# Gate products of the gated recurrence as 64-row products of a half tile each, run for two tiles or for one, some of them in the next pass; weight splits put between the square root and the exponentials

## The chip, the cores and the metric

The kernel runs on one core of a Trainium2 chip. The time is the device time of one execution in microseconds (us), the median over runs. Engines are named as in the profile: PE (matrix products), PEld (PE's weight loads), DVE, ACT, POOL, and the queues SPq and ACTq that issue transfers.

## The reference

One layer of a hybrid decoder for 512 positions and a width of 1024, in float32: a projection of the normalised input, three token mixers beside each other, their gated sum, and a feed-forward block. The change is in the third mixer, the gated recurrence, whose gates are products with 64x64 blocks, one for each of 16 heads:

```python
xc = lax.conv_general_dilated(xr, conv_w[:, None, :], ...) + conv_b
xh = xc.reshape(B, S, RNN_HEADS, RNN_HEAD_DIM)          # 16 heads of 64
r = jax.nn.sigmoid(jnp.einsum('bshi,hio->bsho', xh, w_a).reshape(B, S, RNN_WIDTH) + b_a)
i = jax.nn.sigmoid(jnp.einsum('bshi,hio->bsho', xh, w_x).reshape(B, S, RNN_WIDTH) + b_x)
log_a = -LRU_C * r.astype(jnp.float32) * jax.nn.softplus(-lam.astype(jnp.float32))
a = jnp.exp(log_a)
b_in = jnp.sqrt(-jnp.expm1(2.0 * log_a)) * (i * xc).astype(jnp.float32)
_, h = lax.associative_scan(combine, (a, b_in), axis=1)  # h[t] = a[t] h[t-1] + b_in[t]
return h.astype(xr.dtype) * jax.nn.gelu(gate)
```

## The kernel before, in words

**Numbers in two parts.** Every operand of a product is split into a rounded part `hi` and a remainder `lo` (`split`, L131 on ACT and L136 on DVE), and a product is three products: hi·hi, hi·lo, lo·hi. A *pass* (`passes`, L263) is one tile of 128 output columns for all 512 positions: eight blocks of 128 rows by three, 24 products, into one bank of PSUM. Its weights come by SPq into `raw` (two buffers), are split into `hi` and `lo` (three buffers each), and are fetched two passes ahead (`unit`).

**The recurrence in two halves.** Its 1024 channels are eight tiles of 128, four in each half `b`. For a tile, `xr_tile` makes a pass, then the convolution (`xc`: L499 on ACT, L501 three times on DVE), splits it into `ch` and `cl`, and then makes the gate products (L509): for each of the two gates three products of 128x512, with a weight tile of 128x128 that holds two 64x64 blocks on its diagonal and zeros beside them. Both gates go to banks with the tag `tr`. ACT reads each with one instruction (L511 the sigmoid into `r`, L514 a tanh into `ti`). `rec_batch` then makes for four tiles a tanh (L523), one square root (L524), four exponentials (L530), and on DVE the products and the scan (L539 to L542). The square root and the exponentials need other tables of ACT, each loaded before it. `rec_out` multiplies with the gelu of another pass (`rg_tile`) and splits the outcome into `ych` and `ycl`.

**The order.** The code runs generators: `run` takes the passes one by one; what a tile does behind its pass comes some steps later, in the midst of the following pass; a side generator (`rec_batch`, `rec_out`) is stepped now and then. What is still outstanding is finished at the end of a `run`. A scheduler then puts each engine's instructions in an order, and each engine works through its own in that order. `compress` and `hidden` are the first layer of the compressed keys (L784, 64 products), `c_gate` a pass whose outcome ACT takes with a tanh into `merged` (L1179). Behind these comes `c_stage`: for each pair of output tiles, seven products of blocks (L1273, 84 instructions of 128x256), which go by turns to two banks that ACT has to empty (L1277, L1281, L1284, L1289, L1296) before the next product of that bank may begin. They need sums of the recurrence's outcome and of the weights `raw`, made on DVE and ACT just before.

Of the kernel before, what the change touches and what calls it, by code (L numbers as in the profile page):

```python
# [33 lines left out]
NK = 8  # L34
# [18 lines left out]
def hybrid_block(ctx: ExitStack, tc: tile.TileContext, A, out):  # L53
# [84 lines left out]
    res = {}  # L138
# [4 lines left out]
    def w_in(*tiles):  # L143
# [311 lines left out]


    wab = {}

    def start_wab():
        wab["raw"] = slab("wabr", tag="s1", shape=(2, NK, 128))  # L460
# [14 lines left out]
    yc = {}  # L475
    rec = {}
# [11 lines left out]
    def xr_tile(b, c):  # L488
        if c == 0:
            res["late"] = res["raw"]  # L490
            rec[b] = dict(R=slab("r", tag="y" if b else "m"), GG=slab("gg", tag="m"), TI=slab("ti", tag=("s0", "s1")[b]))
        k = 4 * b + c
        ps = bank("mm")
        yield from matrix(ps, hh, hl)
        xc = row("xc")

        def cw(w):
            return vec[:, V_CW + 8 * w + k:V_CW + 8 * w + k + 1]
        res["xc"] = SC.activation(xc, ps, AF.Identity, scale=cw(3), bias=vec[:, V_CB + k:V_CB + k + 1])  # L499
        for i in (1, 2, 3):  # L500
            res["cv"] = V.scalar_tensor_tensor(xc[:, i:], ps[:, :S - i], cw(3 - i), xc[:, i:], op0=OP.mult, op1=OP.add)  # L501
        yield
        ch, cl = row("ch", F32R), row("cl", F32R)
        split(xc, ch, cl)
        yield 4
        for g, dst in ((0, "R"), (1, "TI")):
            pg = bank("tr")
            for t, (w, x) in enumerate((("hi", ch), ("hi", cl), ("lo", ch))):
                PE.matmul(pg, wab[w][:, g, k, :], x, start=(t == 0), stop=(t == 2))  # L509
            if g == 0:  # L510
                SC.activation(rec[b]["R"][:, c, :], pg, AF.Sigmoid, bias=vec[:, V_BA + k:V_BA + k + 1])  # L511
            else:
                ti = rec[b]["TI"][:, c, :]
                last = SC.activation(ti, pg, AF.Tanh, scale=0.5, bias=half[:, 0, k:k + 1])  # L514
                res["ti"] = last, V.scalar_tensor_tensor(ti, ti, 1.0, xc, op0=OP.add, op1=OP.mult)
            yield

    def rec_batch(b):
        r = rec[b]
        r["T"] = slab("t", tag="s2")  # L520
        for c in range(4):
            k = 4 * b + c
            SC.activation(r["T"][:, c, :], r["R"][:, c, :], AF.Tanh, scale=sp4[:, k:k + 1])  # L523
        root = SC.activation(r["T"], r["T"], AF.Sqrt, scale=1.0 / 16)  # L524

        def exps(cs):
            with tc.issue_after(root.ins):
                for c in cs:
                    a = r["R"][:, c, :]
                    SC.activation(a, a, AF.Exp, scale=spm8[:, 4 * b + c:4 * b + c + 1])  # L530

        exps((0, 1) if b else range(4))
        yield
        for c in range(4):
            k = 4 * b + c
            if b and c == 0:
# [170 lines left out]
    def gate_tile():  # L707
# [8 lines left out]
        SC.activation(s[:64], ps[64:], AF.Copy)  # L716
        V.tensor_add(s[:64], s[:64], ps[:64])
        SC.activation(s[:64], s[:64], AF.Sigmoid)
        yield
        pt = bank("tr")  # L720
        for c in range(4):
            PE.transpose(pt[:, c * 64:(c + 1) * 64], s[:64, c * 128:(c + 1) * 128], ident[:64, :64])
# [1323 lines left out]
            close(0, 3, 2 - n, part)  # L2046


    def run(main, side=None, rate=1.0):


        credit = 0.0
        late = []
        for m in main:
            for w in m:
                for x in late:
# [10 lines left out]
                    if next(side, 0) == 0:  # L2067
                        side = None
            credit += rate
        for _, m in late:  # L2070
            for _ in m:
                pass
        if side is not None:
            for _ in side:
                pass

    def seq(*gens):
        for g in gens:
# [49 lines left out]
    def both_out():  # L2128

        batch = rec_batch(1)  # L2130
        next(batch)
        yield
        yield from after(res["ti"], rec_out(0))
        yield from batch
        yield from rec_out(1)

    def inputs(tile, kv):

        for w in tile:
# [126 lines left out]
```

## Time and profile before

| what | value |
|---|---|
| median of 3 runs | 1090.13 us (1089.93 to 1090.33) |
| the profiled execution's own time | 1089.44 us |
| its span, first to last instruction | 1087.7 us |
| mean granted clock of PE | 0.998 |
| PE busy | 1078.3 us, 99% of the span |
| DVE busy | 883.0 us, 81% |
| ACT busy | 661.7 us, 61% |
| gate products, from first to last | 66.8 to 145.7 us |
| first L1273 | 211.3 us |

The profile comes from one execution. A product's time in it is from its start to its modelled end; products overlap, so what one takes away from the next is read from the distance of their starts. The chain of waits follows the work that ended last back to its start. A shape such as 128*128 behind a product is the part of the array that it uses, 64*128 a product over 64 rows.

### The profile page before, as it was taken

To read this page: it belongs to the slowest core of one execution; us is meant where nothing else is said; L and a number is where in the kernel's file an instruction comes from. 1 tells how busy PE (TensorE), PEld (TensorE's weight loads), DVE (VectorE), ACT (ScalarE), POOL (GpSimd) and SP (SyncE) were. 2 spreads that over 40 slices of the span, in tenths; PEclk is the share of its full clock that TensorE was granted. 3 is DMA by queue.
4 is the path that set the end of the run, shared out by engine and by line. 5 is a ranking of instruction groups with operands and counts; after the bars stand their busy time and mean duration, and the time that the engine had idled before them with its cause. 6 is when DMAs were issued, how large, how long until landed. Compare 5 with 4: busy or idle time off the path is not lost.

```text
span 1087.7 us, 16765 instructions
## 1 busy us (share of the span) xinstructions
PE 1078.3 (99%) x6450; PEld 948.5 (87%) x6450; DVE 883.0 (81%) x1557; ACT 661.7 (61%) x1210; POOL 29.0 (3%) x41
## 2 busy tenths in 40 slices
PE   9999999999999999999999999999999999999997
PEld 7888888999889888898888889988999999998886
DVE  6967779669675899998998887876988888889675
ACT  6757574454444676876777655555666666667542
POOL 0000000000000000000000000000000000022200
PEclk9999999999999999999999999999999999999999
DMA  8332325430322221102111134271323322378902
GB/s 312 113 99 82 97 86 204 178 98 20 117 78 78 78 59 39 59 20 79 59 39 59 58 118 136 72 257 39 117 78 117 117 104 97 130 227 202 191 20 97
DMA packets 35312, 115.07 MB, mean 106 GB/s; under 512 B 3584, under 2 KB 3984, under 8 KB 34336
## 3 DMA queue, kind: packets, MB, share of 16 engines
q1 hardware_dynamic: 28496, 97.01, 27.0%
q0 software_dynamic: 5152, 11.09, 5.0%
q10 hardware_dynamic: 1584, 5.90, 1.4%
q8 instruction: 50, 0.82, 0.3%
q14 instruction: 30, 0.25, 0.1%
HBM read 111.89 MB, written 2.10 MB: 105 GB/s over the span
## 4 chain that ended last, share of the span: by engine, by line
PE 97%; DVE 1%; DMA 0%; issue 0%; ACT 0%; DVEq 0%; SPq 0%; ACTq 0%
PE mm L263 37%; PE mm L1755 18%; PE mm L1273 7%; PE mm L1894 6%; PE mm L625 4%; PE mm L1509 4%; PE o L992 4%; PE sc L954 3%; PE tr L979 3%; PE tr L1894 3%; PE mm L870 2%; PE tr L784 1%; PE tr L509 1%; PE mm L1611 1%; PE tr L685 1%; PE tr L892 1%
## 5 line engine op out<-in xcount | busy, mean ns | idle before, releaser
L263 PE MATMUL mm<-hh,hi 128*128 128x512 f32 x504 | 199.5, 396 | 0.0
L263 PE MATMUL mm<-hh,lo 128*128 128x512 f32 x504 | 197.4, 392 | 0.0
L263 PE MATMUL mm<-hl,hi 128*128 128x512 f32 x504 | 196.9, 391 | 0.0
L136 DVE TENSOR_TENSOR lo<-raw,hi 128x1024 fp32r<-128x1024 f32 (+1 forms) x105 | 121.0, 1153 | 38.4 <-ACT hi L131 35.3
L131 ACT ACTIVATE hi<-raw 128x1024 fp32r<-128x1024 f32 (+1 forms) x105 | 105.3, 1003 | 46.5 <-PE mm L263 17.3
L263 PEld LDWEIGHTS mm<-hh,lo 128*128 128x128 f32 x504 | 94.6, 188 | 19.7
L263 PEld LDWEIGHTS mm<-hl,hi 128*128 128x128 f32 x504 | 94.7, 188 | 18.4 <-issue 0.2
L263 PEld LDWEIGHTS mm<-hh,hi 128*128 128x128 f32 x504 | 94.7, 188 | 18.0 <-PE mm L1273 0.2
L960 ACT ACTIVATE P<-P,ast 128x128 f32<-128x128 f32 (+3 forms) x128 | 70.7, 555 | 23.1 <-DVE ast L958 22.5
L958 DVE CUSTOM_DVE_ANT_0 P<-sc,mask 128x128 f32<-128x128 f32 (+3 forms) x128 | 57.9, 484 | 8.2 <-PE sc L954 7.3
L131 ACT ACTIVATE ph<-tr 128x512 fp32r<-128x512 f32 x80 | 46.9, 592 | 25.9 <-PE tr L979 24.0
L136 DVE TENSOR_TENSOR pl<-tr,ph 128x512 fp32r<-128x512 f32 x80 | 54.4, 685 | 2.7 <-PE o L992 0.9
L954 PE MATMUL sc<-K,q 128*128 128x512 f32 (+2 forms) x192 | 51.0, 368 | 0.0
L1755 PE MATMUL mm<-t,hi 128*128 128x256 f32 x288 | 50.7, 276 | 0.0
L1894 PE MATMUL mm<-hi,u 128*128 128x512 f32 x160 | 50.1, 389 | 0.0
L979 PE MATMUL tr<-ident,P 128*128 128x128 f32 x320 | 48.7, 273 | 0.0
L979 PEld LDWEIGHTS tr<-ident,P 128*128 128x128 f32 x320 | 39.0, 140 | 9.8 <-DVE pl L136 1.0
L136 DVE TENSOR_TENSOR lo<-bs,hi 128x1024 fp32r<-128x1024 f32 x28 | 34.1, 1220 | 11.6 <-ACT hi L131 11.6
L1755 PEld LDWEIGHTS mm<-t,hi 128*128 128x128 f32 x288 | 43.4, 188 | 0.0
L1755 PE MATMUL mm<-fh,hi 128*128 128x256 f32 x144 | 40.0, 278 | 0.0
L1755 PE MATMUL mm<-fh,lo 128*128 128x256 f32 x144 | 39.8, 276 | 0.0
L1755 PE MATMUL mm<-fl,hi 128*128 128x256 f32 x144 | 39.8, 276 | 0.0
(489 smaller groups left out, 2896.6 us busy)
## 6 DMA issues: line engine op xcount, KB each, us to landing
raw<-in_w_in SPq DMA_DIRECT2D x64, 512.0 KB, 3.5
rawp<-in_w_fi SPq DMA_DIRECT2D x20, 1024.0 KB, 5.1
bs<-in_w_fo POOLq DMA_DIRECT2D x20, 512.0 KB, 8.1
raw<-in_w_br SPq DMA_DIRECT2D x14, 512.0 KB, 3.6
w<-in_cw ACTq DMA_DIRECT2D x4, 1024.0 KB, 6.7
raw<-in_w_o SPq DMA_DIRECT2D x8, 512.0 KB, 4.1
bs<-in_w_fo SPq DMA_DIRECT2D x8, 512.0 KB, 8.0
raw<-in_w_v SPq DMA_DIRECT2D x6, 512.0 KB, 4.9
```

Source lines behind the costliest of these rows:

```text
L131: res["hi"] = SC.activation(hi, src, AF.Copy)
L136: res["lo"] = V.tensor_sub(lo, src, f32(hi))
L263: res["mm"] = PE.matmul(ps[:m, n0:n1], w[:, k * 128:k * 128 + m], x[k][:, n0:n1], start=(t == 0), stop=(t == 3 * NK - 1))
L625: res["mm"] = PE.matmul(b[c], x[k][:, c * 128:(c + 1) * 128], w[:, kk * 512:kk * 512 + 512], start=(k == 0 and t == 0), stop=(k == NK - 1 ...
L954: PE.matmul(ps[:, :w * n].rearrange("p (b n) -> p b n", b=w), lhs, K[:, i, brs[0]:brs[-1] + 1, :n], start=(i == 0), stop=(i == 1))
L958: V.tensor_tensor_reduce(out=t, in0=ps[:, b * n:b * n + n], in1=mask[0][:, S - n:], scale=-0.125, scalar=3.0e38, op0=OP.add, op1=OP.min, a ...
L960: SC.activation(t, t, AF.Exp, scale=-1.0, bias=st[:, 0, j, b:b + 1], accum_out=st[:, 1, j, b:b + 1])
L979: PE.transpose(pt[:, j * 128:(j + 1) * 128], self.part(j, br)[:, kt * 128:(kt + 1) * 128], ident)
L992: PE.matmul(po, VV[:, kt, g % 2, br].rearrange("p i d -> p (i d)"), x, start=(br == 0 and kt == 0 and t == 0), stop=(br == 1 and kt == a a ...
L1273: res["mm"] = PE.matmul(ps, u[:, k * 128:k * 128 + 128], v[:, k], start=(start and k == t == 0), stop=(k == 3 and t == 2), skip_group_chec ...
L1755: res["mm"] = PE.matmul(ps, w[:, k * 128:k * 128 + 128], x[:, k], start=(start and k == t == 0), stop=(k == 3 and t == 2), skip_group_chec ...
L1894: PE.matmul(ps, a, b, start=id(ps) not in begun, stop=i == len(ops) - 1, skip_group_check=True)
```

## The change

**Smaller products.** The weight tiles of the gates no longer hold zeros: for each half of 64 channels the blocks of both gates stand beside each other (64 rows, 128 columns), so that one product of 64 rows by 128 columns gives both gates of a half tile. For a tile these are two halves by three products, six instructions as before. The two halves use different halves of the array's rows and go to different banks, tag `mm`. In the first half of the recurrence the products of two tiles are issued together, 12 in a run; in the second half those of the first two tiles are, and those of the third and fourth stand alone, 6 in a run. In both halves the last of them come in the midst of the pass that follows (`keep`: `run` hands on what is outstanding instead of finishing it).

**ACT.** Each gate of each tile is now read by two instructions of 64 partitions. In each half the tanh of the last tiles comes behind the square root. The exponentials come two by two, and the split of a weight is put between the root and them.

**Order of passes.** `cmp_tile(2)` stands in the place of the first `rg_tile` of the second half, which moves behind; the first half's `rec_out` moves forward into the second `run`; the second `c_gate` moves ahead of `hidden(first)`. `w_in` lists the weights accordingly.

```diff
-    w_in(*range(T_XR + 1, T_XR + 8, 2), T_CMP + 1, *range(T_XR + 8, T_XR + 16, 2), *range(T_XR + 9, T_XR + 16, 2),
-         T_CMP + 2, T_CMP + 3)
+    w_in(*range(T_XR + 1, T_XR + 8, 2), T_CMP + 1, *range(T_XR + 8, T_XR + 16, 2), T_CMP + 2, *range(T_XR + 9, T_XR + 16, 2),
+         T_CMP + 3)
...
+    ends = slice(0, 64), slice(64, 128)
...
-        hi = slab("wabh", F32R, "wab", (2, NK, 128), 48)
-        lo = slab("wabl", F32R, "wab", (2, NK, 128), 48)
+        hi = slab("wabh", F32R, "wab", (NK, 128), 48)
+        lo = slab("wabl", F32R, "wab", (NK, 128), 48)
...
-        for k in range(0, NK, 2):
-            split(raw[:, :, k:k + 2], hi[:, :, k:k + 2], lo[:, :, k:k + 2])
-            yield
+        for o in ends:
+            for i in range(2):
+                g = slice(64 * i, 64 * i + 64)
+                split(raw[o, i, :, o], hi[o, :, g], lo[o, :, g])
+                yield
...
-        yield 4
-        for g, dst in ((0, "R"), (1, "TI")):
-            pg = bank("tr")
-            for t, (w, x) in enumerate((("hi", ch), ("hi", cl), ("lo", ch))):
-                PE.matmul(pg, wab[w][:, g, k, :], x, start=(t == 0), stop=(t == 2))
...
+        rec[b]["x"] = rec[b].get("x", []) + [(k, xc, ch, cl)]
+        yield (5 - b) if c == 3 else 3
+        if c in ((0, 2), (0,))[b]:
+            return
+        two = rec[b].pop("x")
+        pg = [[bank("mm") for _ in ends] for _ in two]
+        for t in range(3):
+            for i, (k, xc, ch, cl) in reversed([*enumerate(two)]):
+                w, x = (("hi", ch), ("lo", ch), ("hi", cl))[t]
+                for n, own in enumerate(ends):
+                    with tc.issue_after(res["gate"].ins) if t or n or not i else nullcontext():
+                        res["gate"] = PE.matmul(pg[i][n], wab[w][own, k, :], x[own], start=(t == 0), stop=(t == 2))
+        yield
...
+            if k % 4 == 3:
+                r["root"] = SC.activation(r["T"], r["T"], AF.Sqrt, scale=1.0 / 16)
...
-        exps((0, 1) if b else range(4))
+        exps((0, 1))
...
-    run(xr_tiles(0, gate_tile()))
-    tiles = xr_tiles(1, rg_tile(1, 0))
-    run(four(rg_tile, 0) + [cmp_tile(1)] + tiles[:4], rec_batch(0), 0.45)
...
+    late = run(xr_tiles(0, gate_tile()), keep=True)
+    tiles = xr_tiles(1, cmp_tile(2))
...
+    late = run(four(rg_tile, 0) + [cmp_tile(1)] + tiles[:4], first_half(), 0.45, late, True)
...
-    run([tiles[4], *(rg_tile(1, c) for c in range(1, 4)), cmp_tile(2), inputs(cmp_tile(3), 0),
-         behind(c_gate(0), "x0", "x1"), hidden(first), inputs(c_gate(1), 1)],
-        both_out(), 0.45)
+    run([tiles[4], *four(rg_tile, 1), inputs(cmp_tile(3), 0),
+         c_gate(0), behind(c_gate(1), "x0", "x1"), inputs(hidden(first), 1)],
+        second_half(), 0.45, late)
```

**The first gate products on PE.** Before, they stand between the second and the third pass of the recurrence; `tr_710` and `tr_719` are the two gates of the first tile, `ch_670` and `cl_671` its convolved input in two parts.

```order
L263 MATMUL mm_674<-hh_134,lo_598 128x512
L509 MATMUL tr_710<-ch_670,wabh_529 128x512
L509 MATMUL tr_710<-cl_671,wabh_529 128x512
L509 MATMUL tr_710<-ch_670,wabl_530 128x512
L509 MATMUL tr_719<-ch_670,wabh_529 128x512
L509 MATMUL tr_719<-cl_671,wabh_529 128x512
L509 MATMUL tr_719<-ch_670,wabl_530 128x512
L263 MATMUL mm_725<-hh_133,hi_637 128x512
```

In the changed kernel they stand 18 products into the third pass (`mm_714`), for two tiles; `mm_738` and `mm_739` are the two halves of the first tile, `mm_740` and `mm_741` those of the second.

```order
L263 MATMUL mm_714<-hh_134,lo_638 128x512
L519 MATMUL mm_740<-ch_710,wabh_529 128x512
L519 MATMUL mm_741<-ch_710,wabh_529 128x512
L519 MATMUL mm_738<-ch_670,wabh_529 128x512
L519 MATMUL mm_739<-ch_670,wabh_529 128x512
L519 MATMUL mm_740<-ch_710,wabl_530 128x512
...
L519 MATMUL mm_740<-cl_711,wabh_529 128x512
...
L519 MATMUL mm_739<-cl_671,wabh_529 128x512
L263 MATMUL mm_714<-hh_134,hi_637 128x512
```

The products of two tiles moved together and one pass later, and neighbours in the row belong to different halves of the rows.

**ACT where `c_stage` begins.** Before, `t` are the sums of the recurrence's outcome, `hi_1749` and `hi_1767` sums of weights, `merged` the tanh of the last pass ahead of L1273, `r_273` and `r_274` what empties the two banks of L1273, and `hi_1863` the weights of the first pass behind.

```order
L131 ACTIVATE t_1757<-ti_1073 128x1024
L131 ACTIVATE hi_1749<-raw_1667 128x1024
L131 ACTIVATE hi_1767<-raw_1668 128x512
L793 ACTIVATE chid_1702<-chid_1702 128x2x124
L1179 ACTIVATE merged_1571<-mm_1789 128x512
L1277 ACTIVATE r_273_1817<-mm_1815 128x256
L1281 ACTIVATE r_274_1818<-mm_1816 128x256
L1284 ACTIVATE r_273_1817<-mm_1815 128x256
L131 ACTIVATE hi_1863<-raw_1861 128x1024
```

In the changed kernel `mm_1805` is that last pass, `t_1773`, `hi_1765` and `hi_1783` are the sums, and `hi_1879` and `hi_1936` the weights of the two passes behind.

```order
L1208 ACTIVATE merged_1595<-mm_1805 128x512
L131 ACTIVATE t_1773<-ti_1079 128x1024
L1306 ACTIVATE r_273_1833<-mm_1831 128x256
L131 ACTIVATE hi_1765<-raw_1683 128x1024
L131 ACTIVATE hi_1783<-raw_1684 128x512
L1313 ACTIVATE r_273_1833<-mm_1831 128x256
...
L1310 ACTIVATE r_274_1834<-mm_1832 128x256
...
L1318 ACTIVATE r_274_1834<-mm_1831 128x256
L131 ACTIVATE hi_1879<-raw_1877 128x1024
L1325 ACTIVATE r_274_1834<-mm_1831 128x256
L131 ACTIVATE hi_1936<-raw_1934 128x1024
```

The last of the sums and the weights that belong to them now stand behind `merged` and behind the first emptying of a bank, and `hi_1936` behind the last one.

**PE at the same place.** Before, the seven products go to the banks `mm_1815` and `mm_1816` in long turns of 8 to 15 instructions, and the pass behind them follows undivided.

```order
L1273 MATMUL mm_1815<-ych_1336,lo_1715 128x256
L1273 MATMUL mm_1816<-ych_1584,a12h_1731 128x256
...
L1273 MATMUL mm_1816<-ych_1336,lo_1750 128x256
L1273 MATMUL mm_1815<-t_1740,hi_1714 128x256 x2
...
L1273 MATMUL mm_1815<-t_1764,a22l_1709 128x256
L263 MATMUL mm_1942<-hh_133,hi_1863 128x512
L263 MATMUL mm_1942<-hl_135,hi_1863 128x512
L263 MATMUL mm_1942<-hh_133,lo_1864 128x512
```

In the changed kernel the banks are `mm_1831` and `mm_1832`, and `mm_1958` and `mm_2013` the two passes behind.

```order
L1302 MATMUL mm_1832<-ych_1569,a12l_1748 128x256
L1302 MATMUL mm_1831<-t_1756,hi_1730 128x256 x2
...
L1302 MATMUL mm_1831<-t_1756,lo_1731 128x256
L1302 MATMUL mm_1831<-t_1773,hi_1783 128x256 x2
...
L1302 MATMUL mm_1831<-t_1780,a22l_1725 128x256
L263 MATMUL mm_1958<-hh_133,hi_1879 128x512
L263 MATMUL mm_1958<-hl_135,hi_1879 128x512
L263 MATMUL mm_2013<-hh_133,hi_1936 128x512
L263 MATMUL mm_1958<-hh_133,lo_1880 128x512
```

Three instead of 15 instructions of the other bank stand between the first product of `mm_1831` and its second, none between its second (`t_1756`) and its third (`t_1773`), and one instruction of the pass `mm_2013` has moved into the pass `mm_1958`.

More of the change, by code (lines that the diff above doesn't have):

```diff
@@ L502, in xr_tile @@
         yield
-        ch, cl = row("ch", F32R), row("cl", F32R)
+        ch, cl = row("ch", F32R, "tg"), row("cl", F32R, "q32")
         split(xc, ch, cl)
-        yield 4
-        for g, dst in ((0, "R"), (1, "TI")):
-            pg = bank("tr")
-            for t, (w, x) in enumerate((("hi", ch), ("hi", cl), ("lo", ch))):
[L509 to L515, printed above, removed]
-            yield
+        rec[b]["x"] = rec[b].get("x", []) + [(k, xc, ch, cl)]
@@ new lines, in xr_tile, with act @@
+        yield
+        r = rec[b]
+        def act(out, part, k, own, n):
+            if part == 0:
+                return SC.activation(out[own], n[:64], AF.Sigmoid, bias=vec[own, V_BA + k:V_BA + k + 1])
+            return SC.activation(out[own], n[64:], AF.Tanh, scale=0.5, bias=half[own, 0, k:k + 1])
+        for i, (k, xc, ch, cl) in enumerate(two):
+            for n, own in enumerate(ends):
+                act(r["R"][:, k % 4, :], 0, k, own, pg[i][n])
+        if c < 3:
+            yield
+        else:
+            r["T"] = slab("t", tag="s2")
+            for j in range(4):
+                SC.activation(r["T"][:, j, :], r["R"][:, j, :], AF.Tanh, scale=sp4[:, 4 * b + j:4 * b + j + 1])
@@ new lines, in xr_tile @@
+        for i, (k, xc, ch, cl) in enumerate(two):
+            if k % 4 == 3:
+                r["root"] = SC.activation(r["T"], r["T"], AF.Sqrt, scale=1.0 / 16)
+            ti = r["TI"][:, k % 4, :]
+            for n, own in enumerate(ends):
+                with tc.issue_after(r["root"].ins) if "root" in r else nullcontext():
+                    last = act(ti, 1, k, own, pg[i][n])
+            res["ti"] = last, V.scalar_tensor_tensor(ti, ti, 1.0, xc, op0=OP.add, op1=OP.mult)
+            if c == 1:
+                yield
@@ L518, in rec_batch @@
     def rec_batch(b):
+        while "root" not in rec.get(b, ()):
+            yield
+        yield
         r = rec[b]
[L520 to L524, printed above, removed]
+        ahead = (r["root"], res["hi"])
         def exps(cs):
-            with tc.issue_after(root.ins):
+            with tc.issue_after(ahead[0].ins), tc.issue_after(ahead[1].ins):
@@ L535, in rec_batch @@
             k = 4 * b + c
-            if b and c == 0:
+            if c == 0:
                 exps((2, 3))
@@ L718, in gate_tile @@
         SC.activation(s[:64], s[:64], AF.Sigmoid)
-        yield
+        yield 2
         pt = bank("tr")
@@ L2046, in down, with run @@
             close(0, 3, 2 - n, part)
-    def run(main, side=None, rate=1.0):
+    def run(main, side=None, rate=1.0, late=None, keep=False):
         credit = 0.0
-        late = []
+        late = late or []
         for m in main:
@@ L2069, in run @@
             credit += rate
-        for _, m in late:
-            for _ in m:
+        while late and not keep:
+            for _ in late.pop(0)[1]:
                 pass
@@ L2075, in run @@
                 pass
+        return late
     def seq(*gens):
@@ L2124, in hybrid_block, with first_half, second_half @@
     run([v_half(0), v_half(1), cmp_tile(0)], seq(norm(), load_wab()))
-    run(xr_tiles(0, gate_tile()))
-    tiles = xr_tiles(1, rg_tile(1, 0))
-    run(four(rg_tile, 0) + [cmp_tile(1)] + tiles[:4], rec_batch(0), 0.45)
[L2128 to L2134, printed above, removed]
+    late = run(xr_tiles(0, gate_tile()), keep=True)
+    tiles = xr_tiles(1, cmp_tile(2))
+    def first_half():
+        yield from rec_batch(0)
+        while 1 not in rec:
+            yield
+        yield from rec_out(0)
+    def second_half():
+        yield from rec_batch(1)
         yield from rec_out(1)
+    late = run(four(rg_tile, 0) + [cmp_tile(1)] + tiles[:4], first_half(), 0.45, late, True)
     def inputs(tile, kv):
```

## The prediction

> **What bounds the kernel now.** I read the page first: the span, the busy shares and the shares of the chain of work that ended last.
>
> ```profile
> span 1087.7 us, 16765 instructions
> ...
> PE 1078.3 (99%) x6450; PEld 948.5 (87%) x6450; DVE 883.0 (81%) x1557; ACT 661.7 (61%) x1210; POOL 29.0 (3%) x41
> ...
> PE 97%; DVE 1%; DMA 0%; issue 0%; ACT 0%; DVEq 0%; SPq 0%; ACTq 0%
> ```
>
> PE is the bound. The view of PE's waits says what it ever stood for (total, times, longest):
>
> ```profile
> PE mm L353 <- DVE warm L297: 1.1, 1, 1.1
> PE mm L625 <- DVE gxh L363: 0.5, 1, 0.5
> PE o L992 <- DVE yb L1000: 0.2, 1, 0.2
> ```
>
> That is 1.8 us in all, none of it where the change works. So a microsecond less of products is a microsecond less of time, and a new wait costs its full length; there is next to no old wait to take away. The third view is PE's groups from 60 to 150 us, and the fourth the chain in order of time (start, length, what).
>
> ```profile
> L509 PE MATMUL tr<-ch,wabh 128*128 128x512 f32 x16 | 6.2, 400 | 0.0
> L509 PE MATMUL tr<-cl,wabh 128*128 128x512 f32 x16 | 6.2, 389 | 0.0
> L509 PE MATMUL tr<-ch,wabl 128*128 128x512 f32 x16 | 6.2, 389 | 0.0
> ```
>
> ```profile
> 66.93 1.36 PE tr L509 x6
> ...
> 199.55 6.45 PE tr L784 x56
> 206.00 5.48 PE mm L263 x24
> 211.48 9.57 PE mm L1273 x84
> ```
>
> There are 48 gate products. A product lasts 0.39 us to its modelled end, but the next begins earlier: six take 1.36 us of the chain, 0.227 each, 10.9 us for the eight tiles.
>
> **The products.** After the change there are again 48, each with half the rows. Two neighbours use different halves of the array and write different banks. If they run beside each other, a pair takes one slot: 24 x 0.227 = 5.44 us, a gain of **5.44**. No row of before shows two products beside each other; if they do not overlap, the gain is 0. I take 5.44, as the two share neither rows nor bank; the end at 0 is a rival below.
>
> **The switches.** The products come in five runs (12, 12, 12, 6, 6), each entered from 128-row products and left to them: ten switches. Before has one short stretch on 64 rows, the transposes of L722, read in the timeline of PE and of PEld (start, length; what the engine waited for in brackets):
>
> ```profile
> 86.03 0.39 PE L263 MATMUL mm<-hh,hi 128*128 128x512 f32 x1
> 86.26 0.39 PE L263 MATMUL mm<-hl,hi 128*128 128x512 f32 x1
> ...
> 87.71 0.46 PE L722 MATMUL tr<-ident,gsig 64*128 64x64 f32 x4
> 88.10 0.50 PE L509 MATMUL tr<-ch,wabh 128*128 128x512 f32 x1
> 88.43 0.39 PE L509 MATMUL tr<-cl,wabh 128*128 128x512 f32 x1
> ```
>
> ```profile
> 86.03 0.19 PEld L263 LDWEIGHTS mm<-hl,hi 128*128 128x128 f32 x1
> ...
> 87.71 0.32 PEld L722 LDWEIGHTS tr<-ident,gsig 64*128 64x128 f32 x4 [0.35 <-ACT gsig L718]
> 88.09 0.19 PEld L509 LDWEIGHTS tr<-ch,wabh 128*128 128x128 f32 x1
> ```
>
> Between equal products the load (86.03) begins with the product ahead and is hidden. The first product back on 128 rows has its load at 88.09, only just ahead of it, lasts 0.50 instead of 0.39, and the next stands 0.33 behind it instead of 0.227: about 0.11 lost. The switch into 64 rows can't be read there, since PE waited for ACT. I take 0.11 for each of ten, **+1.1**; the ends are 0, if the transposes' wait made the loss, and 0.2 each (a load of 0.19 wholly bare), +2.0. [...]
>
> **ACT and DVE in the gate stage.** Two gate readings of 128 partitions become four of 64. The rows:
>
> ```profile
> 82.19 0.68 ACT L511 ACTIVATE r<-tr,vec 128x512 f32<-128x512 f32 x1
> 82.76 0.69 ACT L514 ACTIVATE ti<-tr,half 128x512 f32<-128x512 f32 x1
> ...
> 85.55 0.60 ACT L716 ACTIVATE gsig<-mm 64x512 f32<-64x512 f32 x1 [0.97 <-PE mm L712]
> ...
> 91.13 1.28 ACT L524 ACT_TABLE_LOAD   x1
> 92.42 1.92 ACT L524 ACTIVATE t<-t 128x2048 f32<-128x2048 f32 x1
> 94.34 1.28 ACT L530 ACT_TABLE_LOAD   x1
> 95.64 2.56 ACT L530 ACTIVATE r<-r,spm 128x512 f32<-128x512 f32 x4
> ```
>
> Sixteen more readings at about 0.57 (82.76 - 82.19; the row of 64 partitions lasts about as long as one of 128) are +9 us of ACT. ACT has room: PE's waits show none for it here. The tightest place was the square root and the exponentials, 1.28 + 1.92 + 1.28 + 2.56 = 7.0 us in one piece, more than a pass; the change cuts this piece by a weight split behind the root and lets the exponentials come by two. Chaining these rows along the new order, the tightest split (the third pass of the gelu in the first half) is ready about 1.3 us ahead of its product. So 0, with a cover of 1.3 us; a table or a reading that comes later than that costs PE what is beyond it. The number of table loads stays. The weights of the gates are split in as many elements as before: 0. On SP and POOL only the order of the weights' transfers changes, and they too land over a microsecond early: 0.
>
> DVE is tighter. A tile's gates now need `ch` and `cl` at a fixed place in the next pass:
>
> ```profile
> 77.42 1.22 DVE L136 TENSOR_TENSOR lo<-raw,hi 128x1024 fp32r<-128x1024 f32 x1
> 78.55 0.68 DVE L136 TENSOR_TENSOR cl<-xc,ch 128x512 fp32r<-128x512 f32 x1
> ...
> 81.38 2.32 DVE L501 SCALAR_TENSOR_TENSOR xc<-mm,vec,xc 128x511 f32<-128x511 f32 x3 [2.15 <-ACT xc L499]
> ```
>
> For the eighth tile `cl` stands behind a `lo` of 1.22. Counted from the start of the run ahead of it: the run (six in three slots, 0.68), the two products left of the pass (0.227 + 0.39) and the bias on ACT (some 0.8, my estimate from the readings above) make 2.1; the three convolution steps 2.3, a product with `ti` 0.7 (as `cl`), `lo` 1.2, `cl` 0.7 and hand-overs 0.5: ready at 7.5. Its product is due after 0.68 + 28 slots of 0.227 and two switches at 0.11 = 7.25. That is 0.3 us of wait, and at the first run `ch` comes 0.1 late by the same count: **+0.4** (0 to 0.8). If the switches are free the product is due earlier, and the wait is 0.5.
>
> **The start of `c_stage`.** T0 is the start of its first product (211.32 before). Here the order costs time. Rows:
>
> ```profile
> 211.32 0.28 PE L1273 MATMUL mm<-ych,hi 128*128 128x256 f32 x1
> 211.44 0.28 PE L1273 MATMUL mm<-ycl,hi 128*128 128x256 f32 x1
> ...
> 212.62 0.28 PE L1273 MATMUL mm<-ych,lo 128*128 128x256 f32 x1
> ```
>
> ```profile
> 211.29 0.63 ACT L131 ACTIVATE hi<-raw 128x512 fp32r<-128x512 f32 x1 [2.68 <-PE mm L263]
> ...
> 212.13 0.58 ACT L1179 ACTIVATE merged<-mm 128x512 f32<-128x512 f32 x1
> 212.93 0.39 ACT L1277 ACTIVATE r<-mm 128x256 f32<-128x256 f32 x1 [0.22 <-PE mm L1273]
> ...
> 216.35 1.06 ACT L131 ACTIVATE hi<-raw 128x1024 fp32r<-128x1024 f32 x1
> ```
>
> Products stand 0.118 or 0.114 apart (9.57 / 84) and end 0.28 after their start; an emptying takes 0.39 and begins 0.03 after the product's end (212.62 + 0.28 to 212.93). Step by step:
>
> - The second product of the bank `mm_1831` stands three instructions behind the first one's 12: due at T0 + 15 x 0.118 = 1.77. ACT runs `merged` (from T0 + 0.19, 0.58) and a sum (1.05) ahead of the emptying: it starts at 1.62 to 1.66 and is done at 2.05. Wait 0.3.
> - `hi_1765` (1.05) starts behind that emptying and is ready at 3.06; due after eight more instructions at 2.96. Wait 0.1.
> - The third product of `mm_1831` follows the second directly: 0.28 + 0.39 + two hand-overs of 0.03 = 0.73 against 0.11. Wait 0.62.
> - The emptying of `mm_1832` has the same 0.73 covered by five instructions: 0.16.
> - `hi_1936` stands behind the last emptying, which waits for the last L1302: 0.28 + 0.39 + 1.05 = 1.72. Its product is due behind 0.114 and two slots of 0.227 = 0.57. Wait 1.14.
> - `lo_1880` on DVE is late by some 0.2.
>
> Together **+2.5**. The lower end keeps only the third and the fifth, which no order on ACT can shorten: 1.7. The upper end doubles the six hand-overs and adds a second, at most 0.1 each: 3.2. The weights of `hi_1879` are no wait: their transfer goes out when `lo_1766` is done, near T0 + 4.2, and takes 3.7 us, while they are due behind the last L1302 near T0 + 10.8.
>
> ```profile
> raw<-in_w_in SPq DMA_DIRECT2D x11, 512.0 KB, 3.7
> ```
>
> The other moves of passes bring no product more or less: 0 on a PE that doesn't wait.
>
> **Sum.** -5.44 + 1.1 + 0.4 + 2.5 = -1.4 on the profiled execution's own 1089.44: 1088.0. The median of the runs is 0.69 above that execution (1090.13), so **1088.7**. With switches at 0.05 to 0.2 (0.5 to 2.0) and `c_stage` at 1.7 to 3.2 this case reaches from 1088.7 - 0.6 - 0.8 = 1087.3 to 1088.7 + 0.9 + 0.7 = 1090.3. A measurement of this kernel tells about 0.2% from no change, 2.2 us: faster is below 1087.9, slower above 1092.3.
>
> **Rivals.**
>
> *More gain.* The switches are free, the gate stage waits 0.5, and `c_stage` loses only its 1.7: -5.44 + 0.5 + 1.7 = -3.2, **1086.9**. For it: the late load at 88.09 may be the transposes' wait alone. Against it: the load stands after that wait was over.
>
> *Slower: the change doesn't do what it says.* The two halves do not run beside each other; 48 slots of 0.227 stay, and the switches and `c_stage` are paid: 1.1 + 2.5 = +3.6, **1093.7**. It decides by the distance d of the two starts in a pair: the gain is 24 x (0.227 - d), so the change is at zero at d = 0.06 (5.44 - 24 x 0.06 = 4.0, the cost terms) and slower by over 0.2% from d = 0.15 on. For it: no two products overlap in any row of before but by their tail. Against it: different rows, different banks, weights and operands, nothing shared but the stream in. [...]
>
> *Bare loads.* The pair overlaps, but the next pair's loads stand bare, as the transposes' did. Their price:
>
> ```profile
> L722 PEld LDWEIGHTS tr<-ident,gsig x4: 135/138/138, 87.7 to 87.9; 64*128 64x128 f32 x4
> ```
>
> A pair then takes 0.227 + 0.135 = 0.362, 24 of them 8.7: a gain of 2.2 only, and -2.2 + 1.1 + 0.4 + 2.5 = +1.8, **1091.9**. Against it: at 86.03 a load of 128 rows runs beside a product of 128 rows, so nothing in the rows says that it can't. [...]
>
> **How the numbers follow.** Forecast 0.55, more gain 0.22, bare loads 0.10, slower 0.13. A fifth of the forecast's own range lies below 1087.9 (0.6 of 3.0), so faster is 0.22 + 0.2 x 0.55 = 0.33. Slower is 0.13 and 0.02 of the bare loads: 0.15. Same: the rest, 0.52. The range 1086.2 to 1092.2 takes in the first three cases with 0.7 us beyond the better one (its waits at their lowest ends) and leaves out the slower one and a little of each end.
>
> **What would show it.** In the timeline of PE the second product of a pair starts a few ns after the first, and a run of 12 lasts 1.4 to 1.6 us rather than 2.7; the first 128-row product behind it is 0.50 long. PE's waits show L1302 for ACT's L1306 and L1313, L263 for ACT's L131 with about 1.1 near T0 + 11, and L519 for DVE's `cl` with about 0.3. T0 lies near 211.3 - 5.44 + 1.5 = 207.4. I am wrong if a pair stands 0.06 or more apart, if a run's edges cost far more than 0.11, if PE waits for a weight split behind the root, or if `c_stage` begins without waits.

## The result, and the profile after

The changed kernel takes 1104.78 us in the median of 4 runs (1103.29 to 1104.9), the kernel before 1090.23 on the same chip (1089.93 to 1090.7): a ratio of 1.013, interval 1.0112 to 1.0147. It is **14.6 us slower**, 12.6 us above the upper end of the range. The profiled execution took 1104.9 us, its span is 1103.0.

The page after, with the busy shares of PE and the shares of the chain:

```profile
span 1103.0 us, 16796 instructions
...
PE 92%; DVE 4%; ACT 3%; issue 0%; DVEq 0%; ACTq 0%
```

PE still sets the end, but 8% of the chain now goes through other engines. The view of PE's waits says through which (total, times, longest):

```profile
PE mm L519 <- ACT ch L131: 2.9, 1, 2.9
...
PE mm L263 <- ACT hi L131: 0.6, 1, 0.6
PE mm L1302 <- ACT r L1313: 0.5, 1, 0.5
PE mm L519 <- DVE cl L136: 0.3, 1, 0.3
```

The last three are waits that the prediction names. The first isn't there: 2.9 us for `ch`. All waits together are 4 us above those of before, and the time is 15 us longer, so most of the loss is in no wait at all. The chain in order of time finds it, far behind the change (start, length, what, count). The first fence is before, the second after:

```profile
672.10 9.57 PE mm L1273 x84
...
711.75 38.11 PE mm L1509 x168
...
757.17 10.21 PE mm L263 x90
...
772.76 10.88 PE mm L1611 x96
783.64 186.32 PE mm L1755 x1644
```

```profile
678.68 9.89 PE mm L1302 x84
...
719.32 38.12 PE mm L1538 x168
...
764.75 10.61 PE mm L263 x90
...
780.66 11.31 PE mm L1640 x96
791.97 193.63 PE mm L1784 x1644
```

Line L1273 of before is L1302 of after, L1509 is L1538, L1611 is L1640 and L1755 is L1784. The same 1644 products of 128x256 in the last stage take 193.63 instead of 186.32 us: 117.8 ns apart instead of 113.3, without a wait and with a granted clock of 1.00 in both (the mean from 760 to 1080 us). Seven of the eight stages of 84 products lose 0.32 each, the 90 products of L263 behind 757 us lose 0.40. The products of 128x512 (38.11 and 38.12) lose nothing. This is 7.31 + 0.43 + 0.40 + 7 x 0.32 = 10.4 us, more than two thirds of the loss, and the change alters none of these lines.

The pairs did what was forecast. PE's timeline of the first run of gate products, after:

```profile
71.07 0.39 PE L263 MATMUL mm<-hh,lo 128*128 128x512 f32 x1
71.39 0.73 PE L519 MATMUL mm<-ch,wabh 64*128 64x512 f32 x4
71.96 0.62 PE L519 MATMUL mm<-ch,wabl 64*128 64x512 f32 x4
72.42 0.62 PE L519 MATMUL mm<-cl,wabh 64*128 64x512 f32 x4
72.97 0.50 PE L263 MATMUL mm<-hh,hi 128*128 128x512 f32 x1
```

Twelve products from 71.39 to 72.97 are 1.58 us. By the starts in the trace the second of a pair begins 2 to 4 ns behind the first here, and 1 to 13 ns in all 24 pairs.

The third run of gate products, after, shows the wait and what follows it. PE's timeline, then the windows (time, PE busy, PEld, DVE, ACT, POOL, then PE's granted clock, the DMA share and GB/s):

```profile
128.56 0.39 PE L263 MATMUL mm<-hh,lo 128*128 128x512 f32 x1
131.88 0.73 PE L519 MATMUL mm<-ch,wabh 64*128 64x512 f32 x4 [2.93 <-ACT ch L131]
...
135.39 0.63 PE L263 MATMUL mm<-hh,hi 128*128 128x512 f32 x1
135.81 0.63 PE L263 MATMUL mm<-hl,hi 128*128 128x512 f32 x1
```

```profile
120.00:130.00 10.00, 8.95 (x40) 7.09 (x38) 9.97 (x17) 5.53 (x9) 0.00 (x0) 1.00 0.18 53
...
132.00:134.00 2.00, 2.00 (x13) 1.01 (x13) 0.84 (x2) 1.50 (x2) 0.00 (x0) 0.76 0.35 66
134.00:136.00 2.00, 2.00 (x7) 1.61 (x6) 0.00 (x0) 0.68 (x2) 0.00 (x0) 0.50 0.52 205
```

Up to 130 us DVE is busy 9.97 of 10 us. Behind the wait the granted clock falls to 0.50, and products of 128x512 last 0.63 instead of 0.39 and stand 0.43 apart instead of 0.227. The windows of before up to there:

```profile
100.00:110.00 10.00, 10.00 (x46) 8.28 (x45) 10.00 (x14) 5.45 (x8) 0.00 (x0) 1.00 0.49 129
110.00:120.00 10.00, 10.00 (x46) 8.29 (x45) 7.58 (x9) 3.53 (x6) 0.00 (x0) 1.00 0.43 143
120.00:130.00 10.00, 10.00 (x46) 8.29 (x45) 7.50 (x10) 6.75 (x9) 0.00 (x0) 1.00 0.17 52
```

DVE had a quarter of the last window free there. What fills it now is in DVE's timeline of after:

```profile
123.00 0.75 DVE L504 SCALAR_TENSOR_TENSOR xc<-mm,vec,xc 128x511 f32<-128x511 f32 x1
123.67 0.68 DVE L587 TENSOR_TENSOR ti<-ti,gg 128x512 f32<-128x512 f32 x1
124.27 0.74 DVE L504 SCALAR_TENSOR_TENSOR xc<-mm,vec,xc 128x510 f32<-128x510 f32 x1
124.92 0.42 DVE L136 TENSOR_TENSOR ycl<-ti,ych 128x256 fp32r<-128x256 f32 x1
```

Between the steps of a convolution (L504) stand the products and splits of the first half's `rec_out` (L587 and `ycl`), which the change moves into this run: four of 0.69 and four of 0.41, 4.4 us in all. `ch` waits for the last L504.

The half clock did not follow such a wait each time. In the first run of experiment 1, which is the changed kernel with one more product, PE waits 2.98 us at the same place, and the window behind it has the full clock:

```profile
131.42 0.74 PE L519 MATMUL mm<-ch,wabh 64*128 64x512 f32 x4 [2.98 <-ACT ch L131]
```

```profile
132.00:134.00 2.00, 2.00 (x14) 1.26 (x11) 0.37 (x1) 1.35 (x2) 0.00 (x0) 1.00 0.50 129
```

### The profile page after: what moved, and what is told of

Its sections match the earlier page's. It is cut to its first block, busy times and chain, and to the rows that moved or that the text cites. A ratio compares the mean times of both kernels' runs of the same rounds, so it can differ in the third digit from the quotient of the medians.

```text
span 1103.0 us, 16796 instructions
## 1 busy us (share of the span) xinstructions
PE 1089.9 (99%) x6450; PEld 956.1 (87%) x6450; DVE 884.2 (80%) x1557; ACT 674.8 (61%) x1226; POOL 29.7 (3%) x41
## 4 chain that ended last, share of the span: by engine, by line
PE 92%; DVE 4%; ACT 3%; issue 0%; DVEq 0%; ACTq 0%
PE mm L263 32%; PE mm L1784 18%; PE mm L1302 7%; PE mm L1923 6%; PE mm L654 4%; PE mm L1538 4%; PE o L1021 4%; PE sc L983 3%; PE tr L1008 3%; PE tr L1923 3%; PE mm L899 2%; PE tr L813 1%; PE mm L1640 1%; DVE lo L136 1%; PE tr L714 1%; PE tr L921 1%
## 5 line engine op out<-in xcount | busy, mean ns | idle before, releaser
L263 PE MATMUL mm<-hh,hi 128*128 128x512 f32 x504 | 200.8, 398 | 0.7 <-ACT hi L131 0.6
L263 PE MATMUL mm<-hh,lo 128*128 128x512 f32 x504 | 198.1, 393 | 0.0
L263 PE MATMUL mm<-hl,hi 128*128 128x512 f32 x504 | 197.8, 393 | 0.0
L263 PEld LDWEIGHTS mm<-hh,hi 128*128 128x128 f32 x504 | 95.2, 189 | 20.9 <-issue 1.6
L263 PEld LDWEIGHTS mm<-hh,lo 128*128 128x128 f32 x504 | 95.0, 188 | 19.9 <-DVE lo L136 0.2
L263 PEld LDWEIGHTS mm<-hl,hi 128*128 128x128 f32 x504 | 95.1, 189 | 18.5 <-issue 0.6
L1784 PE MATMUL mm<-t,hi 128*128 128x256 f32 x288 | 52.4, 280 | 0.0
L1784 PEld LDWEIGHTS mm<-t,hi 128*128 128x128 f32 x288 | 44.0, 187 | 0.0
L1784 PE MATMUL mm<-fh,hi 128*128 128x256 f32 x144 | 40.6, 282 | 0.0
L1784 PE MATMUL mm<-fl,hi 128*128 128x256 f32 x144 | 40.2, 279 | 0.0
L1784 PE MATMUL mm<-fh,lo 128*128 128x256 f32 x144 | 40.2, 279 | 0.0
```

The source lines that it names most:

```text
L263: res["mm"] = PE.matmul(ps[:m, n0:n1], w[:, k * 128:k * 128 + m], x[k][:, n0:n1], start=(t == 0), stop=(t == 3 * NK - 1))
L1784: res["mm"] = PE.matmul(ps, w[:, k * 128:k * 128 + 128], x[:, k], start=(start and k == t == 0), stop=(k == 3 and t == 2), skip_group_chec ...
```

## The experiments

Each was timed beside the kernel before on the same chip. Two parts of the loss had to be told apart: the pitch of the 128x256 products, and the waits.

**1. Does the pitch go by the count of PE's waits?** It doesn't go by the instructions' order, nor by the banks: behind 650 us both are the same in the two kernels. A first theory was that PE's own instructions that wait, an odd or an even number ahead of the stages, set it. Three kernels, each with one more product, whose outcome is overwritten: after with the first line added, which reads ones; after and before with the second, which reads data that PE waits for anyway, so that a later wait drops out:

```diff
         b = [bank("mm") for _ in range(4)]
+        if f == 0:
+            PE.matmul(b[0][:, :128], ones, ones, start=True, stop=True)
+            PE.matmul(b[0][:, :128], gh[0][:, :128], gh[0][:, :128], start=True, stop=True)
```

> The changed kernel with one more product on PE at the very start (a 128x128 product of the constant ones, its outcome overwritten), which waits for nothing new. It is the control of the next run: two instructions more on PE (load and product), the number of separate wait instructions in PE's queue unchanged (16 ahead of the first product of c_stage). Every theory expects the changed kernel's time, 1104.8 us, to 0.3 us, and 128x256 products 0.118 us apart behind it.

> The same, but the added product reads the first scaled input, so that it takes over the wait that before needed a wait instruction of its own in PE's queue: one instruction less, 15 such waits ahead of c_stage. Theory 'odd or even': the distance of 128x256 products hangs on whether the number of instructions ahead of a load in PE's queue is odd or even; loads and products come in twos, so it is the separate waits that decide (7 in the kernel before, 16 in the changed one). It expects 0.1133 us from the first change of banks of every c_stage on, as before: some 2400 products by 0.0045 us, 10 to 11 us less, 1094 us. Rival 'what 64-row products or half a clock leave behind', and rival 'other addresses of the operands': 1104.8 us, nothing changes.

> The kernel before with that same added product: 6 separate waits ahead of c_stage instead of 7, nothing of the change in it. 'Odd or even' expects 128x256 products 0.118 us apart throughout: 10 to 11 us more than before, 1101 us. The rivals expect 1090.3 us.

Measured: 1104.66 (ratio 1.0133, 1.0118 to 1.0149), 1105.33 (1.0139, 1.0122 to 1.0156) and 1090.28 (1.0002, 0.9993 to 1.0012). The last stage keeps its 193.63 us in both kernels made of after and its 186.32 in the one made of before. **This theory fell.**

**2. Does it go by where the weights lie?** The timeline of before holds a hint. In a stage of 84 products the first twelve stand 0.118 apart, the others 0.1133:

```profile
671.94 0.28 PE L1273 MATMUL mm<-ybh,hi 128*128 128x256 f32 x1
...
673.35 0.28 PE L1273 MATMUL mm<-ybh,a12h 128*128 128x256 f32 x1
...
674.71 0.28 PE L1273 MATMUL mm<-ybh,hi 128*128 128x256 f32 x1
```

Between 671.94 and 673.35 stand twelve products, 1.41 us in all; between 673.35 and 674.71 the next twelve take 1.36 us. The change of pace comes with the first product of `a12h`. The code pads this tile: `row("a12h", F32R, tag, 32)` starts it 32 numbers (128 bytes) into a buffer of 2176 bytes. Two such buffers make a tag, and they lie 8.5 x 256 bytes apart, so with the padding a tile lies on a multiple of 256 bytes in one buffer and 128 bytes off in the other. One line of the change, not in the diff above, takes buffers of these very tags:

```diff
-        ch, cl = row("ch", F32R), row("cl", F32R)
+        ch, cl = row("ch", F32R, "tg"), row("cl", F32R, "q32")
```

After it, the later tiles come out in the other buffers. In the built programs `a12h` starts at bytes 30080 and 34432 of a partition before (both 128 off a multiple of 256) and at 36608 and 32256 after (both multiples). `a12l`, `uh`, `ul` and the last stage's `a22h` and `a22l` are 128 off before and on multiples after, as all other weights of these stages are in both; so in after no weight tile of these products lies off. Built without that line, the changed program has `a12h` at 30080 and 34432 again; the line alone in the program of before leaves all these tiles 128 off, so it needs another part of the change beside it. The test exchanges the paddings, once in after, once in before, and once in after for `a12h` and `a12l` alone:

```diff
-                near = row("uh", F32R, "tg", 0), row("ul", F32R, "q32", 0)
+                near = row("uh", F32R, "tg", 32), row("ul", F32R, "q32", 32)
...
-        w["a12"] = row("a12h", F32R, tag, 32), row("a12l", F32R, tag, 0)
+        w["a12"] = row("a12h", F32R, tag, 0), row("a12l", F32R, tag, 32)
...
-        side = 32 * ((j - HEAD + 1) % 2)
+        side = 32 * ((j - HEAD) % 2)
```

> 'Odd or even' has fallen (the product that takes a wait away changed nothing in either kernel). New theory 'trigger': runs of 128x256 products start 0.118 us apart, and fall to 0.1133 at the first weight tile whose address is 128 bytes off a multiple of 256. In the kernel before the pairs a12h/a12l, uh/ul and the last stage's a22h/a22l lie so, in the changed kernel, where the buffers of these two tags come in another turn, all lie on multiples of 256. This run is the changed kernel with the padding of these six tiles exchanged (32 floats for 0, 0 for 32), so that they are again 128 bytes off; every engine's instructions and their order are the same. 'Trigger' expects 0.1133 us from the same places on as in the kernel before: some 2400 products by 0.0045 us, 10 to 11 us less, 1094 us. Rival 'what 64-row products leave behind on PE': 1104.8 us.

> The kernel before with the same exchange of padding, so that its six tiles lie on multiples of 256 bytes; no other difference. 'Trigger' expects 0.118 us throughout, 10 to 11 us more: 1101 us. 'What 64-row products leave behind': 1090.2 us.

> Of the exchange in the changed kernel only a12h/a12l, which the first eight stages of 84 products use, not uh/ul and a22h/a22l of the feed-forward block. 'Trigger' expects that a stretch of 128x512 products sets the state back and that only these stages get faster, 72 products by 0.0045 us in each of some seven: 2 to 2.6 us less, 1102.4 us, the 1741 products of the last stage still 0.118 us apart. If the state outlives the 128x512 products, as one might also think, 1094 us.

Measured: after with all three edits 1094.54 (ratio 1.0036, 1.0024 to 1.0049), **10.2 us faster**; before with the same edits 1100.35 (1.009, 1.0075 to 1.0105), **10.1 slower**; after with the edit of `a12` alone 1102.87 (1.0114, 1.0099 to 1.0129). The chains of the three, in this order:

```profile
678.21 9.57 PE mm L1302 x84
...
789.75 186.32 PE mm L1784 x1644
```

```profile
673.61 9.89 PE mm L1273 x84
...
786.90 193.63 PE mm L1755 x1644
```

```profile
677.32 9.57 PE mm L1302 x84
...
789.61 193.63 PE mm L1784 x1644
```

The paddings alone carry the pace over from one kernel to the other, to the hundredth of a microsecond. With `a12` alone the stages of 84 are quick (9.57) and the last stage, which has other tiles, stays slow (193.63). So it is shown that in these kernels the place of these weight tiles decided the pace of these stages. By the rows above the products behind them, whose tiles lie on multiples of 256, stood 0.113 apart too. Each of the eight stages of 84 in before, all behind products of 128x512, began with twelve at 0.118 again. And after two larger distances of 0.15 and 0.23 us at 654 us in before, the next 56 products stand 0.118 apart. Before with the exchange has none of the 64-row gate products and is slow, so these have no part in it.

The place of a tile does not account for all of it. Among those 56 products are nine of `a12h` and `a12l` from 658.54 us on, whose tiles lie 128 off, and they stay 0.118 apart; in after with the exchange the same nine go at 0.113. Twelve of `a22h` and `a22l` at 972.55 us in before, all 128 off, stand 0.118 apart too. And in after five products from 216.9 us on stand 0.113 apart though no tile lies off. What else it takes, and why the place of a weight acted on the pace of PE here, no run shows.

**3. Is it `rec_out` on DVE that makes `ch` late?** After with `rec_out(0)` back in the third `run`, where before had it; with the extra product that reads `gh` as in 1, which alone changed nothing:

```diff
-        while 1 not in rec:
-            yield
-        yield from rec_out(0)
...
-        yield from rec_batch(1)
+        batch = rec_batch(1)
+        next(batch)
+        yield
+        yield from after(res["ti"], rec_out(0))
+        yield from batch
         yield from rec_out(1)
```

> The changed kernel with the first half's rec_out back behind the gates of the second half, as before, and the added product of the run above, so that the number of separate waits stays even (14). Theory 'DVE is full': the third run of gate products waited 2.9 us because the multiplications and splits of rec_out (4.4 us) stood on DVE between the convolution steps; without them the wait goes, and with it the 1.95 us that PE lost at half its clock behind it: 1104.8 - 5.0 = 1099.8 us, clock 1.0 throughout. Rival 'half clock comes from the 64-row products, not from the wait': 1101.8 us. Rival 'the wait is ACT's or a transfer's': 1104.8 us. 128x256 products stay 0.118 us apart by 'odd or even'.

Measured: 1102.72 (ratio 1.0119, 1.0104 to 1.0134), 2 us under after, where the theory had 5. Its waits, and a window at the place (same columns as above):

```profile
PE tr L815 <- DVE x L796: 1.1, 1, 1.1
...
PE mm L519 <- ACT ch L131: 0.4, 1, 0.4
```

```profile
132.00:134.00 2.00, 2.00 (x11) 1.65 (x10) 1.50 (x2) 1.96 (x4) 0.00 (x0) 1.00 0.00 0
```

The wait falls from 2.9 to 0.4: it is shown to come from these eight instructions. The clock stays at 1.00 without it, with the 64-row products in place, so these are not what halves it. But a part of the gain is given back 50 us later, where PE now waits 1.1 us for `x` (L815 here is L813 of after, with lines added above it). In after `x` is done at 183.1 us and PE begins with it at 187.6; here the eight instructions stand on DVE ahead of `x`, it is done at 185.1, and PE is there earlier. The other 1.8 of the missing 2.9 us are not accounted for.

**4. The order of the passes ahead of `c_stage`.** After with the exchanged paddings, and then the edit of 3, the old order of passes, or both:

```diff
-         c_gate(0), behind(c_gate(1), "x0", "x1"), inputs(hidden(first), 1)],
+         behind(c_gate(0), "x0", "x1"), hidden(first), inputs(c_gate(1), 1)],
```

> The full exchange of padding in the changed kernel, and the first half's rec_out back behind the gates of the second half. The two causes lie in different stages and should add: 10 to 11 us from the padding, and 2.0 us from rec_out as measured above (the wait for ch and the half clock behind it gone, 1.1 us of a wait at the compressed keys in their place): 1092 us. If 'trigger' is wrong: 1102.7 us.

> The changed kernel with the padding exchanged, and the passes ahead of c_stage in the order of the kernel before (c_gate(0), hidden, c_gate(1)). Theory 'emptying and weights at the start of c_stage': the waits read there in the changed kernel (0.30, 0.64, 0.17, 0.23, 0.79, 0.19, and 0.11 behind most of them, 2.8 us in all) come from that order and go: 1094.5 - 2.8 = 1091.8 us. Rival 'they come from 64-row gates or the later recurrence, whatever stands ahead of c_stage': 1094.5 us.

> All three together: padding exchanged, rec_out back, the passes ahead of c_stage in the old order. If the three causes are all there is and add, 1092.7 - 2.8 = 1089.9 us, still with 1.1 us of a wait at the compressed keys and some 1.3 us at two runs of gate products. If they hide one another, more.

Measured: 1092.66 with the edit of 3 (1.0021, 1.0012 to 1.0031), 1092.09 with the old order (1.0017, 1.0008 to 1.0026) and 1096.48 with both (1.0056, 1.0044 to 1.0069). The old order takes 2.45 us off the 1094.54 of experiment 2, and the waits of L1302 and of L263 for ACT are gone: this is the `c_stage` term. **Both edits together were a miss**: 6.6 us above what was expected. From its waits, and a window behind the first of them:

```profile
PE tr L813 <- DVE x L794: 3.0, 1, 3.0
```

```profile
186.00:188.00 2.00, 2.00 (x12) 2.00 (x11) 2.00 (x3) 0.52 (x1) 0.71 (x1) 0.50 0.20 16
```

The clock is halved behind this wait too: the first 32 products of L813 take 5.30 us, where the next 16 take 1.79. So some 1.7 us of the miss are half clock again; another 1.7 are waits of 0.3 to 0.8 in and behind `c_stage`. As for the cause, with `rec_out(0)` behind the last tanh its eight instructions stand ahead of `x` on DVE, and with the old order there is a pass less between `x` and PE's demand for it. That each edit takes away time that had covered for the other is argued from this order, not tried.

**5. The 64-row products alone.** Before with the gates as two halves, one tile at a time, as ever right behind the pass, in the banks `tr`, with four readings by ACT; no order is changed:

```diff
+        pg = [bank("tr") for _ in ends]
+        for t, (w, x) in enumerate((("hi", ch), ("hi", cl), ("lo", ch))):
+            for n, own in enumerate(ends):
+                PE.matmul(pg[n], wab[w][own, k, :], x[own], start=(t == 0), stop=(t == 2))
```

> Of the change only the 64-row products with their smaller weight tiles and four readings on ACT, one tile at a time, in the order of the kernel before; the six padded tiles lie 128 bytes off as before. 'Pairs overlap, each run costs 0.4 us': -5.44 + 10 runs by 0.41 (eight tiles, two of them cut in two by a product of a pass) = -1.3, 1088.9 us. If runs cost nothing: 1084.8 us. If the pairs' gain is eaten by the switches entirely: 1090.2 us.

Measured: 1091.87 (ratio 1.0016, 1.0007 to 1.0025), 3.0 above what was expected. The pitch of the last stage stays at 186.32 / 1644: the products have no part in it. Its waits show where the 3.0 went:

```profile
PE tr L789 <- issue: 1.2, 1, 1.2
...
PE tr L727 <- ACT gsig L723: 0.7, 1, 0.7
PE mm L263 <- DVE lo L136: 0.6, 1, 0.6
...
PE tr L513 <- ACT ch L131: 0.5, 1, 0.5
```

The sum is 1.2 + 0.7 + 0.6 + 0.5 = 3.0. Three of them stand on ACT or one step behind it (`lo` follows `hi`), and ACT has sixteen more readings; that these make them late is argued, not tried. What released L789 the profile doesn't say. And the eight tiles came as ten runs of 64-row products, at the 0.41 of a run in after (worked out below) some 4.1 us of switches against 5.44 of gain. So by this count the saving is all but used up by the switches where tiles go one at a time, and the grouping by two halves that cost.

**6. A version without all of these.** After with the exchanged paddings, the old order, and `rec_out(0)` released by the split of the last tile's `cl`, into the 7 us in which DVE otherwise waits for the last tanh:

```diff
+        if c == 3:
+            rec[b]["cl"] = res["hi"], res["lo"]
...
-        while 1 not in rec:
-            yield
-        yield from rec_out(0)
...
+        while "cl" not in rec[1]:
+            yield
+        yield from after(rec[1]["cl"], rec_out(0))
         yield from rec_batch(1)
```

> The kernel after with the paddings exchanged and the old order of the passes ahead of the C stage (the run with those two edits had 1092.09 us), and the first batch's gate products and splits (L587 and ycl) moved: they are issued only once the last tile's cl has been split, so that they fall into the 7 us in which VectorE waited for the last tanh (152.6 to 159.6 us in that run). Theory (the wait of 3.0 us for ch at the third run of gate products, and the clock granted at half speed behind it, come only from VectorE being full there with these eight instructions of 4.4 us): the wait falls under 0.6 us, the clock stays at 1.00 in 130-138 us, and the time falls by 3.0 - 0.5 + 1.95 = 4.5 us to 1087.6 us, which would be below the kernel before (1090.2). Rival (the eight instructions crowd whatever they stand beside, as when they were put behind the third run and the C stage): the wait goes and the clock comes back, but TensorE waits 3 to 4 us between 180 and 215 us for the compressed tokens or the first operands of the C stage, and the time stays between 1090.5 and 1092.5 us. Second rival (the wait is set by the chain ch - convolution itself): the wait stays at 2 us or more and the time at 1091 us or above.

Measured: **1089.86** (1088.92 to 1093.86, 11 runs) against 1090.15 (15 runs) of before: a ratio of 1.0, 0.9991 to 1.001. Its waits:

```profile
PE tr L815 <- DVE x L796: 1.0, 1, 1.0
PE mm L521 <- DVE cl L136: 0.5, 1, 0.5
PE mm L521 <- ACT ch L131: 0.4, 1, 0.4
```

The long wait and the half clock are gone, as the theory had it, but only 2.2 us of the 4.5 expected came. The rival was right in kind and not in size: PE now waits 1.0 us for `x`, where the kernel without this edit had 0.2 and the rival had 3 to 4. And one of the runs of six was cut in two by the scheduler, one more pair of switches. The whole change, freed of these losses, is worth nothing that can be measured here. No run beat the kernel before by more than the noise.

## Why the prediction was wrong, point by point

| term | forecast | measured |
|---|---|---|
| pairs beside each other | -5.44 | -5.44 |
| switches | +1.1 | +2.05 |
| `cl` of the last tile | +0.4 | +0.5 |
| start of `c_stage` | +2.5 | +2.9 |
| `ch` at the third run | none | +3.0 |
| half clock behind it | none | +1.65 |
| pitch of the 128x256 products | none | +10.2 |
| sum | -1.4 | +14.9 |

The medians differ by 14.6. The pitch is what the exchange of the paddings gave back; the other rows are read from the starts in the trace of after.

**The pairs: right.** The two halves begin 1 to 13 ns apart, the first run of 12 takes 1.58 us (1.4 to 1.6 forecast). The two rivals that doubted the overlap, *the change doesn't do what it says* and *bare loads*, are both refuted by the same rows.

**The switches: a loss as forecast, the size not.** I read 0.11 from the one switch back of before and gave the switch into the run the same. Around the first run, in the fence above, the first 64-row product stands 0.32 behind its forerunner, 0.09 more than 0.227; its two pairs take 0.57 instead of 0.45; behind the last two pairs, 0.55 instead of 0.45, the first 128-row product comes 0.10 late and lasts 0.50, and the next stands another 0.11 late. That is 0.41 for a run and 2.05 for five, just above the 2.0 that I had as the upper end. It is 0.2 us on each side of a run: the 0.11 of before, which I took for every switch, was about half of it. What PE does in that time the rows don't show.

**`cl` and `c_stage`: right.** PE waited 0.3 for the last `cl`; its product stands 0.43 late, and the one behind it 0.10. In `c_stage` the starts give 0.30 for the emptying (0.3 forecast), 0.64 for the third product (0.62), 0.17 for `mm_1832` (0.16), 0.23 and 0.79 for `hi_1936` (1.14) and 0.19 for `lo_1880` (0.2). What I left out is that the product after a wait is followed 0.11 late, five times here: +0.55. The old order of the passes took 2.45 back. `hi_1765` (0.1) was hardly late at all. Of the tightest weight splits behind the root none was late, as forecast.

**`ch`: the step that failed is that of ACT and DVE in the gate stage.** There I counted the chain for the eighth tile, found 0.3, and put the first run at 0.1. The sentence that the first half's `rec_out` moves forward into the second `run` stood in my description of the change, and none of its 4.4 us of DVE was ever priced. In DVE's windows of before, 10.00, 7.58 and 7.50 of each 10 us are busy from 100 to 130 us: that leaves 4.9 us free, hardly more than the 4.4 that came in, so a late chain through DVE was to be expected there. I wrote that DVE is tighter, and counted it for the first and the last run, not for the third.

**The half clock: not in the sum at all.** I priced a new wait at its full length. The 2.93 us cost another 1.65: 5.06 us lost between 128.56 and 136.57, less 0.41 for the run and 3.0 for the wait. Where the wait was 0.4 the clock stayed at 1.00. It also did once behind a wait of 2.98, so the length of the wait alone did not set this part of the loss; what else did is not shown.

**The pitch: the largest term, and the step that failed most.** I gave the change's other edits 0 because they bring no product more or less, and so took the pitch of all products as given. A line that only names another tag for `ch` and `cl` moved the buffers of instructions that run more than 600 us later, and so 10 us; my description of the change didn't list it. The range had no room for it, since every cost in it was bound to an instruction that the change touches.

## What to carry to other kernels

When a change takes buffers from a tag, ask who else takes from it and whether their padding or parity still holds; compare start addresses in the two built programs, not the instructions alone. When two kernels differ without a wait, lay the chain's pieces with equal counts beside each other, last stage included: 1644 products are a ruler to the tenth of a nanosecond. And price every moved step on every engine, at each place it lands beside, not at the one place that looks tight.

## What the runs showed of the hardware that I had not expected

- Products of 128x256 in fp32r stood at two distances, 117.8 and 113.3 ns, at the same granted clock of 1.00. In before each of the eight stages of 84 began with twelve products at 0.118, and the distance fell to 0.113 at the first product of `a12h`, whose tile starts 128 bytes off a multiple of 256; in seven of them it stayed there for the rest of the stage, over tiles on multiples too. The 90 products of L263 took 10.21 us in before and 10.61 in after, the 1644 of the last stage 186.32 and 193.63. With the paddings exchanged, so that the tiles lay the other way, the last stage took 186.32 in after and 193.63 in before. Experiment 2 has the places where the distance did not go with the place of the tile. 128x512 products showed no such difference (38.11 and 38.12 us for 168).
- PE's granted clock fell to 0.50 behind an idle time of 2.93 us in after, and behind one of 2.98 in the first run of experiment 1 it stayed at 1.00, as it did behind 0.4 in experiment 3. Waits of 3.0 were followed by the half clock in experiment 4 with both edits (0.50 from 186 to 188 us), and in experiment 2 with all three edits in after the mean clock from 100 to 140 us was 0.96, as in after itself. In after the clock stood at 0.50 for 3.41 us, from 133.04 to 136.45 us, between 126.29 us and 962.56 us at 1.00. The length of a wait alone did not decide it in these runs; what else did is not shown.
- At five of the six late products in and behind `c_stage` in after, the one that follows is itself late by about 0.11 us, so a wait that the profile shows as 0.5 (L1302 for L1313) made 0.64 + 0.11 by the starts.
